# Layer 0's experts: an over-full expert changes places with number 17, which runs two blocks on one load of its weights

## The chip, the cores and the metric

The kernel runs on one core of a Trainium2 chip. The metric is the device time of one execution in microseconds (us), as the median of three runs. TensorE (PE) does the matmuls, VectorE (DVE), ScalarE (ACT) and GpSimd (POOL) the rest; SyncE (SP) issues most of the transfers from HBM.

## The reference

A trunk of two layers on 256 latent and 256 context tokens of width 1024. Each layer is a mixer (attention and a state-space scan in layer 0) with a hierarchical mixture of 32 experts behind it. Layer 0's experts see all 512 tokens, layer 1's the 256 latent ones. All is in fp32:

```python
g_prob = softmax(h @ wg + bg)                     # 4 groups of 8 experts
g_gate, g_sel = top_k(g_prob, 1)
e_top, e_idx = top_k(logits of the chosen group, 2)
gate = g_gate * softmax(e_top)
expert = g_sel * 8 + e_idx                        # two experts for each token
...
y[e] = (silu(x @ w1[e]) * (x @ w3[e])) @ w2[e]    # 1024 -> 512 -> 1024
out[token] += gate * y
```

The inputs are drawn with a fixed seed. Worked out from them with the reference's own router, layer 0's 1024 assignments fall on the 32 experts as in the first list, layer 1's 512 as in the second:

```
69 29 42 22 24 49 41 24 33 38 22 30 30 41 34 24 37 41 28 38 45 35 36 28 28 31 20 35 23 18 10 19
1 14 7 9 5 8 8 0 29 8 21 41 6 18 37 22 27 8 7 11 16 36 21 6 12 11 21 9 53 16 9 15
```

## The kernel before

Tokens of one expert are gathered into a block of 64 slots (`CAP`). `moe` runs the experts in order, four to a group; `nt` is the number of token tiles of 128, 4 in layer 0 and 2 in layer 1. For each expert six loads of 1 MiB (halves of `w1` and `w3`, and `w2`) are issued by SP into a ring of twelve buffers (tiles `ringw` and `raw`). PE multiplies (`a`, in `expert_up`), ACT and DVE apply silu and the gate (`sa`, `expert_gate`), PE turns the product (`hp`, `expert_turn`) and multiplies by `w2` (`py`, `expert_down`). The result is split into `yh` (ACT) and `yl` (DVE), and for each pair of experts eight combine steps bring it back to the tokens: PE `pcm`, DVE `ym`, and the add to `S` on POOL or DVE in turn. These steps wait in the list `todo`, those that fetch tokens in `steps`; `fill(n)` issues n of them between the matmuls of the next expert, so the order on PE is written out by hand.

Where a token goes is worked out on DVE. `dest` is its slot among the first 64 of each expert. `route_rest` numbers the overflow blocks, makes `odest` (the slot with overflow counted) and `ov`, a row of integers: the expert of each overflow block, and at the end how many blocks the loop has to run. A group's one-hots (`two`, made from `dq`) select its tokens: PE forms gates and row numbers with them (`pgs`), DVE casts the numbers to `ix`, POOL fetches the `rows` with an indirect load, and PE turns them to `xg`.

The first overflow block of layer 0 is block 32 of the same sequence (`nb = 33`); its expert comes from a register that SP loads from `ov` (L1024), and its gates are made in `block_gates` (`ovd`, `ovg`, eight of each for 512 tokens). Any further block is run by a loop behind the sequence, with a barrier of all engines at either end:

```python
n = nc.values_load(ov[0:1, NOV + 1:NOV + 2], ...)       # L1847
with tc.For_i(0, n, 1) as i:                            # L1848
    e = nc.values_load(ov[0:1, ds(i + 1, 1)], ...)
    oh = self.onehots(ep, nt, self.odest, base, CAP)
    xg, steps = self.turn_rows(ep, self.block_rows(ep, nt, oh), CAP)   # nt == 4
    for step in steps: step()
    c = dict(oh=oh, sl=slice(0, CAP), gs=self.block_gates(ep, nt, base))
    ...
    self.block(ep, layer, tiles, e, xg[:, :, 0, :], c)
```

`block` loads the expert's weights, runs its matmuls and its eight combine steps with nothing else between them. Here n = total - min(total, 1), total being the number of overflow blocks.

Of the kernel before, what the change touches and what calls it, by code (L numbers as in the profile page):

```python
# [32 lines left out]
DM = 1024  # L33
# [5 lines left out]
NOV = 16  # L39

# [27 lines left out]
class Trunk:  # L68
# [338 lines left out]
    def moe_tiles(self, nt):  # L407
        mp = self.moep
        self.h2h = mp.tile([128, nt, 8, 128], F32R, name="h2h")
        self.h2l = mp.tile([128, nt, 8, 128], F32R, name="h2l", tag="h2l", bufs=1)  # L410
        self.lg = mp.tile([128, nt, 36], F32, name="lg")
        self.dest = mp.tile([128, nt, 2], F32, name="dest")
        self.odest = mp.tile([128, nt, 2], F32, name="odest")
        self.gate = mp.tile([128, nt, 2], F32, name="gate")
        self.ov = mp.tile([128, 32], I32, name="ov")

# [573 lines left out]
    def moe(self, layer, tiles):  # L990
# [4 lines left out]
        with ExitStack() as es:  # L995
            with self.pool("exp", "right") as ep:
# [56 lines left out]

                nb = 33 if nt == 4 else 32


                for e in range(nb + 1):
                    cur = cur if e == 0 else begin(e) if e < nb else None
                    if e == 32 and cur:
                        C[16] = B['c']  # L1060
                    elif e % 2 == 0 and e < 32:
                        C[e // 2] = dict(oh=ohs[e // 4], sl=slice(64 * (e % 4), 64 * (e % 4) + 128))
                    if cur and e:
                        self.expert_up(cur, 0)
                    fill(2)

                    fill({1: 0, 2: 2, 3: 2}.get(e, 2 if e > 28 or e % 4 == 1 else 1) if nt == 4 else 2 if e > 28 else 1, steps)
                    if prev:
                        self.expert_turn(prev)
                    if cur:  # L1070
                        self.expert_up(cur, 1)
                    fill(2)
                    if e == 0:
                        gates(0)
                    if e % 4 == 2 and e < 28 and nt == 2:
                        gates(e // 4 + 1)
                    if cur:
                        cur['gs'] = cur['gs']()
                        self.expert_gate(cur)
                    if prev:  # L1080
                        k = (e - 1) % 2
                        c = C[(e - 1) // 2]
                        if k == 0 and e < 33:
                            self.combine_turn(ep, nt, c)
                        self.expert_down(prev, c, k)
                        if k or e == 33:
                            todo += self.combine_steps(ep, tiles, c, CAP if e == 33 else 128)
# [56 lines left out]
    def turn_rows(self, ep, rows, n):  # L1144
# [3 lines left out]
        xg = ep.tile([128, 8, 4, 64], F32, name="xg", bufs=2)  # L1148
# [25 lines left out]
    def group_gates(self, ep, nt, oh, e, rows=None):  # L1174

        gs = ep.tile([64, 4], F32, name="gs", bufs=3)
        for i in range(2):
            pg = self.ps([128, 2, 33], "pgs")
            for t in range(nt):
                self.mmp(pg.rearrange("p a b -> p (a b)"), oh[:, t, 128 * i:128 * i + 128], self.gdr[:, t].rearrange("p a b -> p (a b)"),  # L1180
                         start=(t == 0), stop=(t == nt - 1))
# [410 lines left out]
    def route_rest(self, nt):  # L1592
# [23 lines left out]
        gd = self.ep.tile([128, nt, 32], F32, name="gd")  # L1616
# [8 lines left out]
        V.tensor_copy(self.gdr[:, :, 1, 32], self.tok[:, 0:nt])  # L1625
        V.tensor_scalar(ge, R, float(4 * NSLOT), None, op0=OP.is_ge)
# [14 lines left out]
        inc = inc[1][:, 16:48]  # L1641
        adj = rp.tile([128, 32], F32, name="adj")
        V.tensor_tensor(adj, inc, nov, OP.subtract)
        V.tensor_tensor(adj, adj, self.iota[:, 0:32], OP.subtract)
        V.tensor_scalar(adj, adj, float(CAP), float(NSLOT - CAP - 4 * NSLOT), op0=OP.mult, op1=OP.add)
        V.tensor_tensor(ge, ge, bc(adj), OP.mult)
        V.tensor_tensor(R, R, ge, OP.add)
        self.pick(self.odest, 0, nt, V)
        le = self.ym(self.ep, nt).rearrange("p (b e) -> p b e", e=32)
        V.tensor_tensor(le, inc[:, None, :].to_broadcast([128, NOV, 32]),  # L1650
                        self.iota[:, 0:NOV][:, :, None].to_broadcast([128, NOV, 32]), OP.is_le)
        eid = rp.tile([128, 32], F32, name="eid")
        V.memset(eid, 0.0)
        V.tensor_reduce(eid[:, 0:NOV], le, AX.X, OP.add)
        V.tensor_scalar(eid[:, 0:NOV], eid[:, 0:NOV], 31.0, None, op0=OP.min)

        V.tensor_scalar(eid[:, NOV:NOV + 1], inc[:, 31:32], 1.0, None, op0=OP.min)
        V.tensor_tensor(eid[:, NOV + 1:NOV + 2], inc[:, 31:32], eid[:, NOV:NOV + 1], OP.subtract)
        V.tensor_copy(self.ov, eid)

# [17 lines left out]
    def onehots(self, ep, nt, dest, base, n):  # L1678

        V = self.nc.vector  # L1680
        oh = self.oh_tile(nt)
# [86 lines left out]
    def expert_down(self, E, c, k):  # L1768
# [3 lines left out]
        w = self.wload(E['w2'])  # L1772
# [12 lines left out]
    def block_gates(self, ep, nt, base):  # L1785
# [3 lines left out]
        for t in range(nt):  # L1789
            for k in range(2):  # L1790
                d = ep.tile([128, 1], F32, name="ovd", bufs=2)
# [4 lines left out]
                og = ep.tile([128, CAP], F32, name="ovg", bufs=2)  # L1796
# [6 lines left out]
    def block_first(self, ep, nt):  # L1803
# [3 lines left out]
        def begin():  # L1807
            if nt == 4:
                B['oh'] = self.onehots(ep, nt, self.odest, float(NSLOT), CAP)
# [148 lines left out]
```

## Time and profile before

| | |
|---|---|
| median of 3 runs | 1798.81 us (1796.29 to 1799.51) |
| profiled execution | 1799.8 us |
| its span | 1797.9 us |
| mean granted clock of TensorE | 0.966 |
| busy share of the span | PE 92%, DVE 53%, ACT 29%, POOL 16% |
| moved by DMA | 536.15 MB, mean 298 GB/s |

All times in the rows below are counted from the start of the span. Layer 0's experts take the stretch from about 560 to 1091. A row of a timeline gives start, duration, engine, line of the kernel and operation, with `out<-in` by the kernel's names; a bracket holds the idle time of the engine just ahead of it and what ended it.

### The profile page before, as it was taken

How to read it: one execution, taken by the hardware profiler on the slowest of the kernel's cores; microseconds unless marked ns; L12 is line 12 of the kernel's file. 1: busy time of each engine (PE TensorE's matmuls, PEld its weight loads, DVE VectorE, ACT ScalarE, POOL GpSimd, SP SyncE). 2: the span in 40 equal slices, each digit the busy share in tenths (PEclk: the TensorE clock that was granted, in tenths of full speed). 3: DMA queues.
4: the chain of work that ended last, by engine and by line, in shares of the span. 5: the costliest groups of instructions: out<-in, count | busy, mean ns of one | idle time of the engine just before them, and what ended most of it. 6: DMA issues, size and time to landing. Idle time of an engine off the chain costs nothing. (4 is left out here: it accounts for less than half of the span.)

```text
span 1797.9 us, 21742 instructions
## 1 busy us (share of the span) xinstructions
PE 1662.9 (92%) x8093; PEld 861.7 (48%) x8093; DVE 949.2 (53%) x2065; ACT 517.1 (29%) x1003; POOL 284.0 (16%) x257
## 2 busy tenths in 40 slices
PE   6999999999998999999999995989989999999994
PEld 2665565667455444443434334955544444444441
DVE  2354569777676345554555457865553343333425
ACT  2433446444212111111111113477231111111111
POOL 2210000000012412211221124240020010100101
PEclk8999999999998999999999996999989999999998
DMA  9555465654627999999999961352469999999994
GB/s 327 213 203 196 155 190 170 233 199 115 241 74 271 419 420 420 420 421 420 420 421 421 412 270 63 120 211 86 188 258 421 421 421 421 420 421 421 421 421 162
DMA packets 103070, 536.15 MB, mean 298 GB/s; under 512 B 20656, under 2 KB 24752, under 8 KB 49328
## 3 DMA queue, kind: packets, MB, share of 16 engines
q1 hardware_dynamic: 98032, 519.69, 73.7%
q0 software_dynamic: 4928, 15.02, 2.4%
q8 instruction: 66, 1.08, 0.2%
q14 instruction: 44, 0.36, 0.1%
HBM read 531.36 MB, written 3.30 MB: 297 GB/s over the span
## 5 line engine op out<-in xcount | busy, mean ns | idle before, releaser
L197 PE MATMUL a<-ringw,xg 128*64 128x512 f32 x1584 | 368.8, 607 | 2.0 <-DVE ovbase L1843 1.7
L197 PEld LDWEIGHTS a<-ringw,xg 128*64 128x64 f32 x1584 | 113.5, 140 | 211.6 <-issue 203.5
L1206 DVE TENSOR_TENSOR ym<-pcm,mod 128x512 f32<-128x512 f32 x136 | 90.6, 688 | 167.0 <-PE pcm L197 162.2
L1783 DVE TENSOR_TENSOR yl<-py,yh 64x512 fp32r<-64x512 f32 x130 | 89.5, 688 | 163.3 <-ACT yh L1782 161.7
L1782 ACT ACTIVATE yh<-py 64x512 fp32r<-64x512 f32 x130 | 76.8, 591 | 275.1 <-PE py L197 224.3
L1207 POOL TENSOR_TENSOR S<-S,ym 128x512 f32<-128x512 f32 x68 | 86.4, 1271 | 387.3 <-DVE ym L1206 387.3
L197 PE MATMUL py<-ringw,g 128*64 128x512 f32 x640 | 146.1, 597 | 0.0
L197 PE MATMUL a<-raw,xg 128*64 128x512 f32 x496 | 115.3, 603 | 1.8 <-DMA raw<-in_moe_w_dram 1.8
L216 PE MATMUL adaps<-adw,cs 128*32 128x512 f32 x384 | 96.2, 643 | 14.9 <-DMA adw<-in_ada_w_dram 14.9
L105 PE MATMUL pfm<-hTh,wh 128*128 128x512 f32 x256 | 105.0, 412 | 2.8 <-ACT hTh L99 2.7
L1207 POOL TENSOR_TENSOR S<-S,two 128x512 f32<-128x512 f32 x32 | 40.9, 1278 | 407.7 <-DVE two L1206 407.7
L106 PE MATMUL pfm<-hTh,wl 128*128 128x512 f32 x256 | 103.2, 403 | 0.0
L107 PE MATMUL pfm<-hTl,wh 128*128 128x512 f32 x256 | 100.7, 398 | 0.0
L1757 ACT ACTIVATE sa<-a 64x512 f32<-64x512 f32 x65 | 38.4, 591 | 208.9 <-PE a L197 208.9
L197 PE MATMUL pcm<-yh,ohT 128*128 128x512 f32 (+1 forms) x200 | 91.5, 458 | 6.6 <-DVE ym L1206 4.5
L197 PE MATMUL py<-raw,g 128*64 128x512 f32 x400 | 91.3, 598 | 0.5 <-ACT g L1766 0.5
L1206 DVE TENSOR_TENSOR two<-pcm,S 128x512 f32<-128x512 f32 x64 | 42.7, 689 | 92.1 <-PE pcm L197 91.6
L197 PEld LDWEIGHTS py<-ringw,g 128*64 128x64 f32 x640 | 43.7, 136 | 81.2 <-issue 74.2
L197 PEld LDWEIGHTS pcm<-yh,ohT 128*128 128x128 f32 (+1 forms) x200 | 38.2, 191 | 91.4 <-issue 64.8
L197 PE MATMUL pcm<-yl,ohT 128*128 128x512 f32 (+1 forms) x200 | 80.8, 404 | 0.6 <-DVE yl L1783 0.6
L1758 DVE SCALAR_TENSOR_TENSOR sa<-sa,gs,a 64x512 f32<-64x512 f32 x64 | 47.9, 749 | 56.5 <-ACT sa L1757 55.1
L1207 DVE TENSOR_TENSOR S<-S,ym 128x512 f32<-128x512 f32 x68 | 66.5, 978 | 1.8
(519 smaller groups left out, 2754.5 us busy)
## 6 DMA issues: line engine op xcount, KB each, us to landing
ringw<-in_moe_w_dram SPq DMA_DIRECT2D x278, 1024.0 KB, 18.8
raw<-in_moe_w_dram SPq DMA_DIRECT2D x112, 1024.0 KB, 18.4
adw<-in_ada_w_dram SPq DMA_DIRECT2D x96, 512.0 KB, 5.3
raw<-in_w_in_dram SPq DMA_DIRECT2D x18, 1024.0 KB, 8.2
bc<-atd SPq DMA_DIRECT2D x16, 512.0 KB, 6.7
raw<-in_w_out_dram SPq DMA_DIRECT2D x4, 1024.0 KB, 5.6
raw<-in_o_w_out_dram SPq DMA_DIRECT2D x4, 1024.0 KB, 5.9
bias<-in_rpb_dram SPq DMA_DIRECT2D x8, 256.0 KB, 3.8
```

The costliest lines, as they stand in the source:

```text
L105: mm(out, ah, bh, start=start, stop=False)
L106: mm(out, al, bh, start=False, stop=False)
L107: mm(out, ah, bl, start=False, stop=stop)
L197: return self.tc.keep_in_program_order(self.nc.tensor.matmul(*args, **kw))
L216: self.nc.tensor.matmul(p[32 * g:32 * g + 32, :], self.cs[:, j, :], w[:, (g - g0) * 512:(g - g0 + 1) * 512], start=(j == 0), stop=(j == 7))
L1206: nc.vector.tensor_tensor(m, p, self.rows5[t // 2][:, k], OP.mult)
L1207: (nc.gpsimd if i % 2 == 0 else nc.vector).tensor_tensor(S[:, t, k], S[:, t, k], m, OP.add)
L1757: self.nc.scalar.activation(s, a[0:64, :], AF.Silu)
L1758: self.nc.vector.scalar_tensor_tensor(s, s, E['gs'], a[64:128, :], op0=OP.mult, op1=OP.mult)
L1782: nc.scalar.activation(c[h][0][r], py[q], AF.Copy)
L1783: V.tensor_tensor(c[h][1][r], py[q], c[h][0][r], OP.subtract)
```

## The change

In layer 0 the sequence has 32 experts again, and number 17 is run on two blocks with one load of its weights (`twice`). If one of the experts 4 to 31 is over-full, `swap` exchanges it with number 17: the slots, the gates and, through the row `perm`, the weights that are loaded, so the loads of experts 4 to 31 take their address from a register. The overflow block that 17 runs is the exchanged expert's; the others are numbered behind it. If none of them is over-full, `z` is 1, nothing is exchanged, and all overflow blocks are left to the loop. The 33rd load is dropped. The groups' one-hots behind the first take `odest`, which now comes out of `route_rest` with the exchange in it. The second block's tokens are prepared at experts 9 to 12, with one buffer for `ovd` and `ovg`, and all combine steps in `todo` are issued at e = 19.

```diff
-                    ohs[q] = self.onehots(ep, nt, self.dest, 256.0 * q, 256) if q else self.oh0
+                    ohs[q] = self.onehots(ep, nt, self.odest if nt == 4 else self.dest, 256.0 * q, 256) if q else self.oh0
...
                 def begin(e):
-                    if e == 32:
-                        at = nc.values_load(self.ov[0:1, 0:1], engines=[mybir.EngineType.SP], min_val=0, max_val=31)
-                        return self.expert_begin(ep, layer, None, B['xg'][:, :, 0, :], lambda: B['gs'], load=self.expert_at(layer, at))
-                    return self.expert_begin(ep, layer, e, X[e // 4][:, :, e % 4, :], lambda: gs[e // 4][:, e % 4:e % 4 + 1])
+                    load = None
+                    if nt == 4 and e >= 4:
+                        at = nc.values_load(self.perm[0:1, e:e + 1], engines=[mybir.EngineType.SP], min_val=4, max_val=31)
+                        load = self.expert_at(layer, at)
+                    return self.expert_begin(ep, layer, e, X[e // 4][:, :, e % 4, :], lambda: gs[e // 4][:, e % 4:e % 4 + 1], load)
...
-                nb = 33 if nt == 4 else 32
+                nb, twice = 32, None
...
-                    fill({1: 0, 2: 2, 3: 2}.get(e, 2 if e > 28 or e % 4 == 1 else 1) if nt == 4 else 2 if e > 28 else 1, steps)
+                    fill({1: 0, 2: 2, 3: 2, 9: 3, 10: 3, 11: 3, 12: 3}.get(e, 2 if e > 28 or e % 4 == 1 else 1) if nt == 4 else 2 if e > 28 else 1, steps)
...
-                    fill(2)
+                    fill(len(todo) if twice and e == TWICE + 2 else 2)
...
+                        if prev is twice:
+                            c, k, n = B['c'], 0, CAP
...
-                    if e == 27:
+                    if e == (8 if nt == 4 else 27):
...
+                    if e == TWICE and nt == 4:
+                        twice = dict(cur, xg=B['xg'][:, :, 0, :], gs=B['gs'])
+                        self.expert_up(twice, 0)
+                        fill(2)
+                        self.expert_turn(prev)
+                        self.expert_up(twice, 1)
+                        fill(2)
+                        self.expert_gate(twice)
+                        self.expert_down(prev, C[e // 2], 1)
+                        todo += self.combine_steps(ep, tiles, C[e // 2])
+                        twice['w', 2] = prev['w', 2]
+                        prev = twice
...
+        if nt == 4:
+            self.swap(adj, nov, total, gd, nt)
...
+        if nt == 4:
+            V.tensor_copy(eid[:, NOV + 1:NOV + 2], total[:, 1:2])
...
+    def swap(self, adj, nov, total, gd, nt):
+        nc, V, rp = self.nc, self.nc.vector, self.rp
+        it = self.iota[:, 0:32]
+        mx, z, x, dl = (rp.tile([128, 1], F32, name=n) for n in ("swm", "swz", "swx", "swd"))
+        df = rp.tile([128, 32], F32, name="swf")
+        ix, A, Bm, pm = (self.D[:, 1, i] for i in range(4))
+        V.memset(ix[:, 0:4], 0.0)
+        V.scalar_tensor_tensor(ix[:, 4:32], nov[:, 4:32], 1.0, it[:, 4:32], op0=OP.min, op1=OP.mult)
+        V.tensor_reduce(mx, ix, AX.X, OP.max)
+        V.tensor_scalar(z, mx, 0.0, None, op0=OP.is_equal)
+        V.scalar_tensor_tensor(x, z, float(TWICE), mx, op0=OP.mult, op1=OP.add)
+        V.tensor_scalar(adj, adj, z, None, op0=OP.add)
+        V.tensor_tensor(total[:, 1:2], total[:, 0:1], z, OP.add)
+        V.tensor_scalar(total[:, 1:2], total[:, 1:2], -1.0, None, op0=OP.add)
+        V.tensor_scalar(A, it, x, None, op0=OP.is_equal)
+        V.scalar_tensor_tensor(df, it, float(TWICE), A, op0=OP.is_equal, op1=OP.subtract)
+        V.tensor_scalar(dl, x, float(-TWICE), None, op0=OP.add)
+        self.move = rp.tile([128, 32], F32, name="swv")
+        V.tensor_scalar(self.move, df, dl, None, op0=OP.mult)
+        V.tensor_tensor(pm, self.move, it, OP.add)
+        V.tensor_copy(self.perm, pm)
+        V.tensor_scalar(self.move, self.move, float(CAP), None, op0=OP.mult)
+        V.tensor_scalar(A, df, -1.0, 0.0, op0=OP.mult, op1=OP.max)
+        V.tensor_scalar(Bm, df, 0.0, None, op0=OP.max)
+        bc = lambda a: a[:, None, :].to_broadcast([128, nt, 32])
+        gx, g17 = (rp.tile([128, nt], F32, name=n) for n in ("swgx", "swg17"))
+        t = self.D[:, 0]
+        V.tensor_tensor(t, gd, bc(A), OP.mult)
+        V.tensor_reduce(gx, t, AX.X, OP.add)
+        V.tensor_copy(g17, gd[:, :, TWICE])
+        V.tensor_tensor(ix, df, df, OP.mult)
+        V.tensor_scalar(ix, ix, -1.0, 1.0, op0=OP.mult, op1=OP.add)
+        V.tensor_tensor(gd, gd, bc(ix), OP.mult)
+        for m, g in ((A, g17), (Bm, gx)):
+            V.tensor_tensor(t, bc(m), g[:, :, None].to_broadcast([128, nt, 32]), OP.mult)
+            V.tensor_tensor(gd, gd, t, OP.add)
+        self.gdr = self.ep.tile([128, nt, 2, 33], F32R, name="gdr1")
+        nc.scalar.activation(self.gdr[:, :, 0, 0:32], gd, AF.Copy)
+        V.tensor_tensor(self.gdr[:, :, 1, 0:32], gd, self.gdr[:, :, 0, 0:32], OP.subtract)
...
-            E['w', i] = [self.whalf(w[:, 4 * i:4 * i + 4]) for w in E['w13']]
+            if ('w', i) not in E:
+                E['w', i] = [self.whalf(w[:, 4 * i:4 * i + 4]) for w in E['w13']]
...
-                d = ep.tile([128, 1], F32, name="ovd", bufs=2)
+                d = ep.tile([128, 1], F32, name="ovd", bufs=1)
...
-                og = ep.tile([128, CAP], F32, name="ovg", bufs=2)
+                og = ep.tile([128, CAP], F32, name="ovg", bufs=1)
```

VectorE (DVE) where the experts start, before: `dq` and the one-hots `two` of group 1 are among the first rows behind `dest`.

```order
L1684 TENSOR_SCALAR dq<-dest 128x8 x2
L1619 TENSOR_TENSOR gd<-gd,raw 128x128
L1731 COPY xg<-pg 128x512
L1843 MEMSET ovbase 128x1
L1636 SCALAR_TENSOR_TENSOR raw<-raw 128x32
L1662 TENSOR_SCALAR two_4472<-iota,dq 128x256 x4
L1636 SCALAR_TENSOR_TENSOR raw<-raw 128x32
L1623 TENSOR_TENSOR gdr<-gd,gdr 128x4x32
L1663 SCALAR_TENSOR_TENSOR two_4472<-iota,dq,two_4472 128x256 x4
```

And now, at the end of `route_rest`:

```order
L1202 TENSOR_REDUCE gs<-pgs 64x1 x2
L1684 TENSOR_SCALAR raw<-raw 128x16
L1606 TENSOR_REDUCE odest<-raw 128x2x4
L1839 SCALAR_TENSOR_TENSOR sa<-sa,gs,a_4366 64x512
L1685 TENSOR_SCALAR raw<-raw 128x16
L1764 TENSOR_SCALAR dq<-odest 128x8 x2
L1876 TENSOR_SCALAR ovd<-odest 128x1
L1202 TENSOR_REDUCE gs<-pgs 64x1 x2
L1692 CAST ov<-raw 128x32
L1742 TENSOR_SCALAR two_4509<-iota,dq 128x256 x4
L1880 TENSOR_SCALAR ovg<-iota,ovd,gate 128x64
L1743 SCALAR_TENSOR_TENSOR two_4509<-iota,dq,two_4509 128x256 x4
```

The one-hots of group 1 moved from a place ahead of `route_rest`'s small rows to one behind `odest`, with `sa` of expert 0, `gs` and `ov` ahead of them; between the copy of `xg` from `pgb` and `odest` there are by the order some 19 rows more than before. On PE the `pgs` of group 1 stands where it stood, ahead of expert 1's `a`.

PE where expert 18 is run down, before (`a` of expert 19, two combine steps of a `yh` and a `yl` row each, `poT`, and `py`):

```order
L197 MATMUL a_6205<-raw,xg 64x512 x8
L197 MATMUL pcm<-yh,ohT 128x512
L197 MATMUL pcm<-yl,ohT 128x512
L197 MATMUL pcm<-yh,ohT 128x512
L197 MATMUL pcm<-yl,ohT 128x512
L201 MATMUL poT<-ident,two_5528 128x128 x4
L197 MATMUL py_6277<-raw,g 64x512 x8
```

And now, at e = 19, where twenty `pcm` rows in pairs of `yh` and `yl` stand between `a` and `poT`, all alike:

```order
L199 MATMUL a_6556<-raw,xg 64x512 x8
L199 MATMUL pcm<-yh,ohT 128x512
L199 MATMUL pcm<-yl,ohT 128x512
L199 MATMUL pcm<-yh,ohT 128x512
L199 MATMUL pcm<-yl,ohT 128x512
...
L203 MATMUL poT<-ident,two_5716 128x128 x4
L199 MATMUL py_6676<-raw,g 64x512 x8
```

Ten combine steps stand where two stood; behind them there are none on PE until e = 21. On SP 28 register reads of `perm` are added (a TENSOR_LOAD and two small instructions each), most of them among the first loads behind expert 1's.

## Rows read from the trace of the kernel before

**Rows 1.** The table of stretches: for each, time and count per engine, granted clock, DMA share, GB/s.

```profile
600.00:660.00 60.00, 57.89 (x276) 24.66 (x270) 29.69 (x51) 11.02 (x20) 11.10 (x9) 1.00 1.01 421
...
1062.00:1092.00 30.00, 21.21 (x69) 9.44 (x68) 24.13 (x32) 3.35 (x6) 11.45 (x9) 0.79 0.05 20
```

**Rows 2.** PE's waits from 600 to 1060: total us, times, longest.

```profile
PE pg L201 <- DVE ym L1206: 8.4, 23, 0.4
PE pgs L197 <- DVE gs L1186: 6.1, 6, 1.0
PE pgs L197 <- DVE ovg L1797: 1.5, 3, 1.1
```

**Rows 3.** Tile `ringw`, SP's issues between 976 and 979.5, and their time to landing.

```profile
L430 SPq DMA_DIRECT2D ringw<-in_moe_w_dram x2: 328/328/328, 976.6 to 979.0; - x2
...
DMA to landing us min/median/max: 19.7/19.7/19.8
```

**Rows 4.** PE's timeline from 1000: start, duration, line, operation.

```profile
1001.51 1.89 PE L197 MATMUL a<-ringw,xg 128*64 128x512 f32 x8
```

**Rows 5.** DVE's timeline at the end of layer 0's experts.

```profile
1087.15 1.27 DVE L1207 TENSOR_TENSOR S<-S,ym 128x512 f32<-128x512 f32 x1
...
1089.65 1.26 DVE L1207 TENSOR_TENSOR S<-S,ym 128x512 f32<-128x512 f32 x1
1093.08 4.84 DVE L843 BATCH_NORM_STATS2 lnst<-S 128x6 f32<-128x512 f32 x8 [2.17 <-issue]
```

**Rows 6.** DVE's timeline at their start; in brackets the idle time before.

```profile
561.78 1.14 DVE L1662 TENSOR_SCALAR two<-iota,dq 128x256 fp32r<-128x256 f32 x4
...
563.14 1.66 DVE L1663 SCALAR_TENSOR_TENSOR two<-iota,dq,two 128x256 fp32r<-128x256 f32 x4
...
568.24 1.10 DVE L1640 TENSOR_TENSOR raw<-raw 128x32 f32<-128x32 f32 x5
...
573.46 0.34 DVE L1186 TENSOR_REDUCE gs<-pgs 64x1 f32<-64x2 f32 x2 [1.26 <-PE pgs L197]
```

**Rows 7.** Tile `rows`: the indirect loads of token rows.

```profile
DMA to landing us min/median/max: 8.1/10.2/12.4
```

**Rows 8.** PE's timeline at block 32's gates.

```profile
1007.28 0.39 PE L197 MATMUL pgs<-one,ovg 128*64 128x2 f32 x4 [0.86 <-DVE ix L1134]
...
1009.44 0.50 PE L197 MATMUL pgs<-one,ovg 128*64 128x2 f32 x4 [0.21 <-DVE ovg L1797]
1010.15 0.50 PE L197 MATMUL pgs<-one,ovg 128*64 128x2 f32 x4 [0.20 <-DVE ovg L1797]
```

**Rows 9.** PE's timeline in the steady part.

```profile
826.91 3.65 PE L197 MATMUL a<-raw,xg 128*64 128x512 f32 x16
830.50 0.50 PE L197 MATMUL pcm<-yh,ohT 128*128 128x512 f32 x1
...
831.53 0.60 PE L201 MATMUL poT<-ident,two 128*128 128x128 f32 x4
```

**Rows 10.** PE's timeline at the start of the experts.

```profile
561.81 3.68 PE L197 MATMUL a<-ringw,xg 128*64 128x512 f32 x8 [1.71 <-DVE ovbase L1843]
...
576.34 0.60 PE L197 MATMUL pgs<-gdr,two 128*128 128x66 f32 x4 [1.79 <-DVE gs L1186]
...
578.20 5.15 PE L197 MATMUL a<-ringw,xg 128*64 128x512 f32 x16
```

**Rows 11.** PE's timeline behind the last `a`.

```profile
1066.33 0.50 PE L197 MATMUL pcm<-yh,ohT 128*128 128x512 f32 x1 [0.69 <-ACT yh L1782]
...
1070.51 3.65 PE L197 MATMUL py<-ringw,g 128*64 128x512 f32 x16
```

**Rows 12.** Tile `ov`: SP's register reads at the start (ns min/median/max, start).

```profile
L1024 SPq TENSOR_LOAD <-ov x1: 479/479/479, 574.6 to 574.6; - x1
L1847 SPq TENSOR_LOAD <-ov x1: 278/278/278, 575.4 to 575.4; - x1
```

**Rows 13.** SP's waits from 560 to 600.

```profile
SPq L430 <- PE a L197: 30.3, 5, 13.9
```

More of the change, by code (lines that the diff above doesn't have):

```diff
@@ L39 @@
 NOV = 16
+TWICE = 17
 class Pinned:
@@ L415, in moe_tiles @@
         self.ov = mp.tile([128, 32], I32, name="ov")
+        self.perm = mp.tile([128, 32], I32, name="perm")
     def rload(self, src):
@@ L1080, in moe @@
                     if prev:
[L1081 removed]
+                        k, n = (e - 1) % 2, 128
                         c = C[(e - 1) // 2]
[L1083 to L1084 removed]
+                        if prev is twice:
+                            c, k, n = B['c'], 0, CAP
+                        if k == 0:
+                            self.combine_turn(ep, nt, c, n)
                         self.expert_down(prev, c, k)
[L1086 to L1087 removed]
+                        if k or n == CAP:
+                            todo += self.combine_steps(ep, tiles, c, n)
                     if e == 0:
@@ L1142, in next_rows, with turn_rows @@
         return self.rows[:, self.rows_n]
-    def turn_rows(self, ep, rows, n):
+    def turn_rows(self, ep, rows, n, xg=None):
         nc, V = self.nc, self.nc.vector
         k = n // 64
-        xg = ep.tile([128, 8, 4, 64], F32, name="xg", bufs=2)
+        xg = ep.tile([128, 8, 4, 64], F32, name="xg", bufs=2) if xg is None else xg
         def step(jp):
@@ L1615, in route_rest @@
         g2, ge = (rp.tile([128, nt, 32], F32) for _ in range(2))
-        gd = self.ep.tile([128, nt, 32], F32, name="gd")
+        gd = self.ym(self.ep, nt)[:, 0:32 * nt].rearrange("p (t e) -> p t e", t=nt)
         V.tensor_tensor(gd, oh[:, 0], gate[:, :, 0:1].to_broadcast([128, nt, 32]), OP.mult)
@@ L1642, in route_rest @@
         adj = rp.tile([128, 32], F32, name="adj")
-        V.tensor_tensor(adj, inc, nov, OP.subtract)
+        V.tensor_scalar(adj, inc, inc[:, 31:32], -1.0, op0=OP.subtract, op1=OP.mult)
+        total = rp.tile([128, 2], F32, name="ovn")
+        V.tensor_copy(total[:, 0:1], inc[:, 31:32])
+        if nt == 4:
+            self.swap(adj, nov, total, gd, nt)
+        ends = rp.tile([128, 32], F32, name="ends")
+        V.tensor_tensor(ends, adj, nov, OP.add)
         V.tensor_tensor(adj, adj, self.iota[:, 0:32], OP.subtract)
@@ L1645, in route_rest @@
         V.tensor_scalar(adj, adj, float(CAP), float(NSLOT - CAP - 4 * NSLOT), op0=OP.mult, op1=OP.add)
+        if nt == 4:
+            V.tensor_tensor(adj, adj, self.move, OP.subtract)
         V.tensor_tensor(ge, ge, bc(adj), OP.mult)
         V.tensor_tensor(R, R, ge, OP.add)
+        if nt == 4:
+            V.tensor_tensor(R, R, bc(self.move), OP.add)
         self.pick(self.odest, 0, nt, V)
         le = self.ym(self.ep, nt).rearrange("p (b e) -> p b e", e=32)
-        V.tensor_tensor(le, inc[:, None, :].to_broadcast([128, NOV, 32]),
+        V.tensor_tensor(le, ends[:, None, :].to_broadcast([128, NOV, 32]),
@@ L1659, in route_rest @@
-        V.tensor_copy(self.ov, eid)
+        V.tensor_scalar(eid[:, 0:NOV], eid[:, 0:NOV], -1.0, 31.0, op0=OP.mult, op1=OP.add)
+        V.tensor_scalar(eid[:, 0:NOV], eid[:, 0:NOV], 0.0, None, op0=OP.max)
+        if nt == 4:
+            V.tensor_copy(eid[:, NOV + 1:NOV + 2], total[:, 1:2])
+        else:
+            V.tensor_scalar(eid[:, NOV:NOV + 1], total[:, 0:1], 1.0, None, op0=OP.min)
+            V.tensor_tensor(eid[:, NOV + 1:NOV + 2], total[:, 0:1], eid[:, NOV:NOV + 1], OP.subtract)
@@ L1771, in expert_down @@
         g = E['g']
-        w = self.wload(E['w2'])
+        if ('w', 2) not in E:
+            E['w', 2] = self.wload(E['w2'])
+        w = E['w', 2]
         py = self.ps([128, 512], "py2")
@@ L1808, in begin @@
             if nt == 4:
-                B['oh'] = self.onehots(ep, nt, self.odest, float(NSLOT), CAP)
+                B['oh'] = self.onehots(ep, nt, self.odest, float(NSLOT), CAP, ep.tile([128, nt, CAP], F32R, name="ohB"))
                 return
@@ L1814, in rows @@
         def rows():
-            B['xg'], B['steps'] = self.turn_rows(ep, self.block_rows(ep, nt, B['oh']), CAP)
+            B['xg'], B['steps'] = self.turn_rows(ep, self.block_rows(ep, nt, B['oh']), CAP,
+                                                 self.moep.tile([128, 4 * DM], F32, name="xgB", tag="h2h", bufs=1)[:, 0:512]
+                                                 .rearrange("p (j a s) -> p j a s", j=8, a=1))
         def rest():
```

21 lines of the change are left out of this document (10 added, 11 removed).

## Prediction

> **What bounds the kernel now.** The change touches the stretch from 560 to 1091 us, layer 0's experts. I read the table of stretches first. In the steady part the DMA share is 1.01 and 421 GB/s move, while PE is busy 57.89 of 60 [rows 1]: two resources look full at once. Which of them binds is read from PE's waits. From 600 to 1060 PE waited 8.4 us for VectorE's `ym`, 6.1 for `gs` and 1.5 for `ovg`; the two rows left out are DVE's as well, 1.1 together [rows 2]. No row names a DMA. So the weight stream is just fast enough and is never waited for, and PE, one expert after the other, sets the time. How close it is: the tightest pair of loads is issued at 976.6 and 979.0 and takes at most 19.8 [rows 3], so it lies in SBUF by 998.8; its matmuls start at 1001.51 [rows 4], 2.7 later. In the last 30 us of the stage 20 GB/s move and PE is busy for 21.2 [rows 1]: there the combine steps of the last experts run at VectorE's pace.
>
> **The change, part by part.** *The dropped load.* Six loads of 1 MiB (6.29 MB) at 421 GB/s [rows 1] are 14.9 us of DMA time. PE waits for none of it, and the sequence keeps 33 blocks (17 twice in place of number 32), so PE's work stays. Worth 0; the bound on the other side, -14.9, is a rival below.
>
> The Trainium skill ("Perfetto Trace Analysis", Identifying the Most-Contended Engine) says to optimize the resource with the highest use first, here the DMA; by it the sum would hold -14.9 for this term. PE's waits speak against it: the trace shows a full resource that nobody waits for.
>
> *What the exchange does with these inputs.* swap() sets candidates 0 to 3 to zero and takes the largest index among the over-full experts from 4 to 31. The counts of layer 0 (above) have one expert over 64: number 0, with 69; the next has 49. So `mx` is 0, `z` is 1, the exchange is the identity, and expert 17's second block holds no token but is computed all the same. The overflow numbers are shifted by one, and the loop's count is total + z - 1 = 1 + 1 - 1 = 1. Before, expert 0's second block was block 32 in the overlapped sequence and the loop's count was 0: the last add ends at 1089.65 + 1.26 = 1090.91, only the skipped loop's barrier follows, and the next layer's first VectorE work starts at 1093.08 [rows 5]. After, layer 0 computes 32 blocks, an empty one, and one in the loop that stands alone behind a barrier.
>
> *The price of one turn of the loop.* Nothing in the trace runs it, so I build it from like rows in the order of its code, with nothing overlapped but its weights:
> - one more all-engine barrier like the 2.17 at the skip [rows 5]: 2.2 (1 to 4.4);
> - eight one-hot operations of width 64, `pgs`, `ix`: the 256-wide ones take 1.14 and 1.66 for four [rows 6], 2.8 in all; narrower here, but with PE and `ix` behind them, an estimate of 2.9 (2 to 4);
> - the gather of the rows, 8.1 to 12.4 from issue to landing [rows 7]; for 64 rows on an idle DMA the smallest, 8.1;
> - eight transposes and their copies, an estimate of 2.2 (2 to 4);
> - the gates: eight `ovg`, each with a matmul. With two buffers two of them take 1010.15 - 1009.44 = 0.71 [rows 8], 0.35 each. With one buffer PE's read and VectorE's write alternate; I take about twice that, 0.78: 6.2 (2.8 to 8);
> - `ovgs` and `poT`: 1.1 (1 to 2);
> - 32 rows of `a`: sixteen take 3.65 in the steady part [rows 9]; behind a wait eight take 3.68 [rows 10], half the rate. So 7.3 at one level of the clock and 14.7 at the other; PE idles through most of the loop, so a mix, 9.8;
> - activation, gate and `hp`, from engine to engine, an estimate of 2.4 (2 to 3); `py` 3.65 [rows 11];
> - eight combine steps: VectorE's own `S` adds, one for two steps, start 2.50 apart (1087.15 to 1089.65) [rows 5], so 10.0 for eight, with the first wait of 0.69 [rows 11], its `yl` and the last add 12.5 (11 to 15).
>
> The six loads start at the barrier too; at 421 GB/s they take 15 and land before the gates end at about 21, so they hide. Sum 51; all low bounds give 41, all high ones 71.
>
> The Trainium skill ("Runtime: NRT & Kernel Launch", Instruction fetch mechanics) says that a taken branch out of the fetched window makes its engine wait for a fetch. No row here shows a turn of a loop; it would move the 51 toward its top.
>
> *The start.* Group 1's one-hots (1.14 + 1.66) started at 561.78, beside expert 0's matmuls [rows 6]. They now need `odest`, which by the order stands behind some 19 more small VectorE rows. Five such rows take 1.10 [rows 6], so +3.8; DVE idled 1.26 ahead of the `gs` at 573.46 [rows 6], right before `odest`, so 2.5 of it is seen and `odest` ends near 576.4. Then `sa`, `dq`, `gs` and `ov` (about 1.6) and the one-hots with an `ovg`: the last at about 581. PE's `pgs` of group 1, at 576.34 before, waits for them, its last pair ends at about 581.7, and only then can expert 1's `a` start, 578.20 before [rows 10]: +3.5 (2 to 6, the upper end with another stretch of half clock behind the longer wait). All of PE's work is queued behind it, so it is paid in full.
>
> *SP's register reads.* 29 reads, 28 of them new. The two shown start 0.8 apart [rows 12], so 23 us of SP in all. SP waited 30.3 us there for PE to free ring buffers, up to 13.9 at once [rows 13], and a read needs no buffer. Worth 0; if that cover is gone, a rival.
>
> *One buffer for `ovd` and `ovg`.* Block B's gates move to experts 9 to 12. Seven intervals × (0.78 - 0.35) = +3.0, less the 0.86 that PE waited there for `ix` [rows 8], which other work now fills: +2.2 (-1 to +4).
>
> *The flush at e = 19.* Ten combine steps in a row on PE. In the steady part two steps take 831.53 - 830.50 = 1.03 [rows 9]; at VectorE's pace two take 2.5 [rows 5]. Ten would lose 7.4; the first few find free buffers: +4.5 (0 to 7.4).
>
> *The tail.* From the end of the last `py` (1070.51 + 3.65 [rows 11]) to 1090.91 there were 12 steps in 16.8; now 8: 0.7 + 0.7 + 10.0 + 1.8 = 13.2. The four steps cost 4 × 0.515 = 2.1 further ahead: -1.5 (-3 to 0).
>
> Without the loop: 3.5 + 0 + 2.2 + 4.5 - 1.5 = +8.7 (-2 to +17). With it about +59.7.
>
> **The rivals.** (a) *The loop does not run*: the chip's router would have to give expert 0 five assignments fewer. The skipped loop before fits one overflow block or none, so the trace alone doesn't settle it; the counts do. Then +8.7 alone, about 1807. (b) As (a), and flush, gates and start find cover: within 0.2% (3.6 us), about what timing this kernel can tell. (c) *The dropped load pays*, the faster side: if PE keeps pace with the stream, 14.9 come back, about 1784 where the loop isn't run either. It decides from the point where the margin of 2.7 is gone and PE waits for weights; [rows 2] show no such wait. Should it pay and the loop run, the time is about 1843, inside my range. (d) *SP's reads starve the stream at the start*: if half of their 23 came through, 1870; SP's 30.3 of waiting speaks against it.
>
> **How the numbers follow.** The sum is made on the profiled execution, 1799.8, which is 1.0 above the median of 1798.8: 1799.8 + 8.7 + 51 - 1.0 = 1858. The low ends, -2 and 41, give 1838, the high ones, +17 and 71, give 1887; as a range 1836 to 1886. The loop runs: 0.87, nearly all of it inside the range, (d) too. (a) 0.06, (b) 0.03, (c) 0.04. Slower 0.93, same 0.03, faster 0.04.
>
> **What the profile would show.** Right: behind the last `S` add of the sequence one more block, with a gather and six loads at its start, 32 `a` matmuls, and PE idle for most of some 50 us. Group 1's `pgs` waits several us for `two` at the start; the DMA share falls at the end of the stage, while PE's waits still name DVE. Wrong: no `a` between the last add and layer 1 (a); PE waits gone that named a DMA (c), or such a wait come at the start (d); a turn far below 41, where its engines overlap more than the order of the code says.

## The result and the profile after

The changed kernel takes 1847.7 us (median of 4 runs, 1846.69 to 1848.99) where the kernel before took 1797.8 beside it: the ratio is 1.028, with an interval of 1.0265 to 1.0296, so about 50 us slower. Its profiled execution has a span of 1847.1. The prediction was 1858, with a range of 1836 to 1886.

The table of stretches of the changed kernel answers to [rows 1]:

```profile
600.00:660.00 60.00, 57.88 (x272) 24.96 (x270) 31.68 (x61) 11.04 (x20) 11.43 (x10) 1.00 1.01 420
...
1062.00:1092.00 30.00, 26.60 (x104) 11.54 (x100) 20.79 (x29) 4.92 (x9) 8.92 (x7) 0.93 0.77 289
1092.00:1150.00 58.00, 27.01 (x107) 13.16 (x106) 32.49 (x78) 9.61 (x17) 15.54 (x12) 0.65 0.21 72
```

The steady part is as full as before. What is new is the last row: 58 us, the last 14 of them already the next layer's, in which PE is busy for 27, at a mean granted clock of 0.65, and 72 GB/s move. PE's waits from 600 to 1060 answer to [rows 2]:

```profile
PE pg L203 <- DVE ym L1222: 7.4, 20, 0.4
PE pgs L199 <- DVE gs L1202: 5.3, 6, 1.0
PE pgs L199 <- DVE ovg L1880: 4.4, 7, 1.6
PE pcm L199 <- DVE ym L1222: 2.9, 5, 0.8
PE pg L203 <- DVE xg L1177: 1.2, 1, 1.2
PE pg L203 <- DMA rows<-h2d,ix: 0.9, 1, 0.9
```

Again no row names a load of weights; waits for `ovg` grew from 1.5 to 4.4 and `pcm` waits for `ym` have come up. DVE's timeline at the end of layer 0's experts answers to [rows 5]:

```profile
1093.20 1.26 DVE L1223 TENSOR_TENSOR S<-S,ym 128x512 f32<-128x512 f32 x1
1094.38 0.15 DVE L1766 TENSOR_TENSOR dq<-odest,ovbase 128x8 f32<-128x8 f32 x1
...
1135.06 1.26 DVE L1223 TENSOR_TENSOR S<-S,ym 128x512 f32<-128x512 f32 x1
1136.72 4.84 DVE L846 BATCH_NORM_STATS2 lnst<-S 128x6 f32<-128x512 f32 x8 [0.41 <-DVE S L1223]
```

Between the last add of the sequence (1093.20 + 1.26 = 1094.46) and the next layer's first VectorE work lie 42.3 us, where the kernel before had 2.2. Behind the add comes a `dq` made from `ovbase`: the loop's first instruction, with no idle time ahead of it. The count of the loop is 1, as forecast. PE in that turn:

```profile
1095.88 0.76 PE L199 MATMUL pgs<-gdr,two 128*64 128x2 f32 x4 [3.67 <-DVE two L1743]
1100.88 0.70 PE L203 MATMUL pg<-ident,rows 64*128 64x64 f32 x4 [4.25 <-DMA rows<-h2d,ix]
...
1102.37 0.37 PE L199 MATMUL pgs<-one,ovg 128*64 128x2 f32 x2
...
1107.83 0.37 PE L199 MATMUL pgs<-one,ovg 128*64 128x2 f32 x2 [0.41 <-DVE ovg L1880]
...
1109.43 8.16 PE L199 MATMUL a<-ringw,xg 128*64 128x512 f32 x32
...
1120.29 3.65 PE L199 MATMUL py<-ringw,g 128*64 128x512 f32 x16 [0.53 <-ACT g L1847]
1124.64 0.50 PE L199 MATMUL pcm<-yh,ohT 64*128 64x512 f32 x1 [0.69 <-ACT yh L1865]
```

Read from above: PE waits for the one-hots, then for the rows' gather; the gate matmuls (one `ovg` each) stand 0.78 apart; 32 `a` rows take 8.16 and nothing waits for weights. Two more rows, SP's issues and the time of `rows` to landing in that stretch, show a gather that is quick and weights that are there:

```profile
1076.73 4.24 SPq L433 DMA_DIRECT2D ringw<-in_moe_w_dram  x6
```

```profile
DMA to landing us min/median/max: 3.7/3.7/3.7
```

SP went into the loop 18 us ahead of DVE and issued the six loads from 1076.73 to 1080.5; the slowest took 16.5 to landing, so they had landed when POOL started the gather at 1097.1. The gather took 3.7 to landing, where [rows 7] had 8.1 at the least. That the free DMA is the reason is tested below, with two turns of the loop.

### The profile page after: what moved, and what is told of

Its sections match the earlier page's. It is cut to its first block, busy times and chain, and to the rows that moved or that the text cites. A ratio compares the mean times of both kernels' runs of the same rounds, so it can differ in the third digit from the quotient of the medians.

```text
span 1847.1 us, 22468 instructions
## 1 busy us (share of the span) xinstructions
PE 1693.2 (92%) x8193; PEld 875.1 (47%) x8193; DVE 974.0 (53%) x2147; ACT 521.2 (28%) x1011; POOL 289.5 (16%) x262
## 5 line engine op out<-in xcount | busy, mean ns | idle before, releaser
L1222 DVE TENSOR_TENSOR ym<-pcm,mod 128x512 f32<-128x512 f32 x144 | 95.7, 687 | 157.8 <-PE pcm L199 152.9
L1223 POOL TENSOR_TENSOR S<-S,ym 128x512 f32<-128x512 f32 x72 | 91.7, 1273 | 416.6 <-DVE ym L1222 416.6
L199 PE MATMUL py<-ringw,g 128*64 128x512 f32 x656 | 150.0, 597 | 0.5 <-ACT g L1847 0.5
L199 PE MATMUL pcm<-yh,ohT 128*128 128x512 f32 (+1 forms) x208 | 97.0, 466 | 10.6 <-DVE ym L1222 7.5
L199 PE MATMUL pcm<-yl,ohT 128*128 128x512 f32 (+1 forms) x208 | 85.7, 412 | 0.8 <-DVE yl L1866 0.8
L1223 DVE TENSOR_TENSOR S<-S,ym 128x512 f32<-128x512 f32 x72 | 71.4, 992 | 2.1
```

The lines of the kernel that those rows point to most:

```text
L199: return self.tc.keep_in_program_order(self.nc.tensor.matmul(*args, **kw))
L1222: nc.vector.tensor_tensor(m, p, self.rows5[t // 2][:, k], OP.mult)
L1223: (nc.gpsimd if i % 2 == 0 else nc.vector).tensor_tensor(S[:, t, k], S[:, t, k], m, OP.add)
```

## The experiments

**The loop's count set to 0** (expert 0's second block is left out).

```diff
-            V.tensor_copy(eid[:, NOV + 1:NOV + 2], total[:, 1:2])
+            V.memset(eid[:, NOV + 1:NOV + 2], 0.0)
```

> The change with the loop's count set to 0, so expert 0's second block is left out. Theory (the one turn of the loop is the loss): the trace of the change has 42.3 us from the last S add of the sequence to layer 1's first VectorE work, where the kernel before has 2.2, so 40 come back: 1847.7 - 40 = 1807 to 1809, still 9 to 11 above the kernel before. Rival (the sequence itself became slower through register addresses, the empty block and the flush, and most of the loop was covered): less than half comes back, 1828 or more. Rival (the dropped load pays, and only the loop hid it): below 1798.

Measured: 1807.2, ratio to the kernel before 1.0046 (1.0029 to 1.0063). 40.5 us came back (42 by the two ratios), what the trace showed; 5 to 11 are left for everything else in the change.

**Reversed labels**: the exchange takes place, and the loop is not run.

```diff
-        load = load or (lambda n: self.I[n][layer, e])
+        load = load or (lambda n: self.I[n][layer, 31 - e])
...
-        V.tensor_copy(self.perm, pm)
+        V.tensor_scalar(self.perm, pm, -1.0, 31.0, op0=OP.mult, op1=OP.add)
...
-    o['router'] = f(np.concatenate([g('moe_wg'), g('moe_we')], 2).reshape(...))
+    o['router'] = f(np.concatenate([g('moe_wg')[..., ::-1], g('moe_we')[..., ::-1]], 2).reshape(...))
...
```

> The change with the experts' labels counted from 31 down (router columns reversed, weights of label l read from expert 31 - l), so that the over-full expert has label 31, the exchange with 17 takes place and the loop's count is 0; the whole result is computed. Theory: what the exchange moves costs nothing by itself, and the time is that of the loop's count set to 0: 1807 to 1809. Rival (an exchange that takes place costs more than an identity, through other weights or a longer chain to the gates): 1812 or more. Rival (the dropped load pays once the second block is real): below 1798.

Measured: 1806.8, ratio 1.0047 (1.0028 to 1.0065), the same as with the loop's count at 0. An exchange that takes place costs what an identity costs, within these intervals. It also shows the change as it was meant, with 32 loads and 33 blocks: it is still slower than the kernel before.

**33 loads again** (reversed labels): the second block drops the weights it was given and loads its own.

```diff
-                        twice = dict(cur, xg=B['xg'][:, :, 0, :], gs=B['gs'])
+                        twice = {k: v for k, v in dict(cur, xg=B['xg'][:, :, 0, :], gs=B['gs']).items() if not isinstance(k, tuple)}
...
-                        twice['w', 2] = prev['w', 2]
```

> The kernel with reversed labels, but the second block of 17 loads its expert's weights once more, so that 33 loads are made as before. Theory (the DMA stream is full but PE waits for none of it): the time of reversed labels, within 3 us. Rival (PE keeps pace with the stream, so each load is worth its DMA time): 6 loads of 2.5 us more, +15.

Measured: 1811.5 (1805.66 to 1816.34), ratio 1.0058 (1.0036 to 1.0080) against 1.0047; the medians are 4.6 apart, outside the 3 of the theory, the ratios 2. Two later pairs ask the same: 1.0044 against 1.0030, where the exchange is left out as well, and 1.0264 against 1.0246. The kernels with 33 loads come out 0.1 to 0.2% slower, 2 to 3 us, with intervals that overlap in each pair; 15 is excluded. No wait for weights shows on PE in layer 0's experts in any of them.

The traces of this pair show that the load isn't what separates them. From the first `a` to the last add, layer 0's experts take 535.2 with 32 loads and 542.6 with 33, but the difference has arisen before expert 17 is reached, where the two kernels are alike; behind it nothing more is added. Part of it stands at the gates of a group, with 32 loads and then with 33:

```profile
756.72 0.60 PE L199 MATMUL pgs<-gdr,two 128*128 128x66 f32 x4 [0.70 <-DVE gs L1202]
...
757.87 3.65 PE L199 MATMUL a<-ringw,xg 128*64 128x512 f32 x16
```

```profile
762.42 1.03 PE L199 MATMUL pgs<-gdr,two 128*128 128x66 f32 x4 [0.70 <-DVE gs L1201]
...
764.05 6.05 PE L199 MATMUL a<-ringw,xg 128*64 128x512 f32 x16
```

Behind the same wait of 0.70 the sixteen `a` take 3.65 at a granted clock of 1.00 in one execution and 6.05 at 0.60 in the other. In the second pair the traces' difference, 3.7 at expert 16, is also there before expert 17 and stays 3.7 to the end. In the third, PE's waits for gathers are 42.8 with 33 loads and 38.5 with 32; whether the load makes that difference stays open.

**Two turns of the loop**, the second over a block without tokens.

```diff
-            V.tensor_copy(eid[:, NOV + 1:NOV + 2], total[:, 1:2])
+            V.tensor_scalar(eid[:, NOV + 1:NOV + 2], total[:, 1:2], 1.0, None, op0=OP.add)
```

> The change with one more turn of the loop, over an overflow block that holds no token. Theory: a turn costs what the first one shows, about 42 us from its start to its last S add; its weights are issued at the back edge and not ahead of the barrier, but land in 15 to 20 while gather, gates and a take 15 to 23, so +42 to +48: 1890 to 1896. Rival (the weights of the first turn were hidden by being issued 17 us early; without that the a matmuls wait for them): +50 or more, with a PE wait of a for a DMA.

Measured: 1906.1, +58.4 in one run. DVE's timeline at the back edge (the jump from the end of one turn to the start of the next) and at the end, and PE's in the second turn:

```profile
1137.58 1.26 DVE L1223 TENSOR_TENSOR S<-S,ym 128x512 f32<-128x512 f32 x1
1143.84 0.17 DVE L1766 TENSOR_TENSOR dq<-odest,ovbase 128x8 f32<-128x8 f32 x1 [5.00 <-PEq L1935]
...
1192.26 1.26 DVE L1223 TENSOR_TENSOR S<-S,ym 128x512 f32<-128x512 f32 x1
```

```profile
1145.35 0.76 PE L199 MATMUL pgs<-gdr,two 128*64 128x2 f32 x4 [8.78 <-DVE two L1743]
1155.20 0.70 PE L203 MATMUL pg<-ident,rows 64*128 64x64 f32 x4 [9.09 <-DMA rows<-h2d,ix]
...
1163.75 9.56 PE L199 MATMUL a<-ringw,xg 128*64 128x512 f32 x32
...
1176.02 5.12 PE L199 MATMUL py<-ringw,g 128*64 128x512 f32 x16 [0.54 <-ACT g L1847]
```

From the first turn's last add (1137.58 + 1.26 = 1138.84) to the second's (1192.26 + 1.26 = 1193.52) it is 54.7, where the first turn took 41.8. The 12.9 are in the rows: 5.0 idle at the back edge, 9.09 instead of 4.15 for the gather, which now shares the DMA with six loads issued at the same time, and `a` and `py` longer by 1.4 and 1.5, at mean granted clocks of 0.74 and 0.71 where the first loop's turn in the changed kernel had 0.87 and 1.00. Both theories missed: the size is the rival's, but PE doesn't wait for weights; the loads delay the gather.

**Gate operands in one tile** (reversed labels; all eight products, then all eight matmuls).

```diff
...
-                og = ep.tile([128, CAP], F32, name="ovg", bufs=1)
...
+        og = self.ym(ep, nt)
+        for j in range(2 * nt):
+            t, k = divmod(j, 2)
+            V.tensor_scalar(og[:, 64 * j:64 * j + 64], self.iota[:, :CAP], d[:, t, k:k + 1], self.gate[:, t, k:k + 1], ...)
+        for j in range(2 * nt):
+            self.mmp(pg, og[:, 64 * j:64 * j + 64], self.one2, ...)
...
```

> The kernel with reversed labels; the eight gate operands of a block stand side by side in one tile (a ym buffer) and not in one ovg buffer after the other, and one subtraction makes all offsets. Theory: the waits of pgs for ovg were 4.4 us in layer 0 and 2.8 in layer 1, each with some 1.5 of half clock behind it, and the kernel before had about 2.6 and 1.5 of them: about 6 less than reversed labels, 1800 to 1802. Rival (the wait only moves, to ym, which the combine steps need): within 2 us of reversed labels, 1805 to 1809.

Measured: 1808.2, ratio 1.0048 (1.0029 to 1.0067), no gain; the rival holds. PE at the gates in this kernel:

```profile
735.08 1.75 PE L199 MATMUL pgs<-one,ym 128*64 128x2 f32 x16 [2.59 <-DVE ym L1879]
...
737.87 4.78 PE L199 MATMUL a<-raw,xg 128*64 128x512 f32 x16
```

One wait of 2.59 stands in place of seven, and the burst behind it still takes 4.78 where 3.65 is the steady value [rows 9]. VectorE finishes the operands too late, however they are stored.

**Spread steps** (reversed labels; no flush).

```diff
-                    fill(len(todo) if twice and e == TWICE + 2 else 2)
+                    fill(3 if twice and TWICE + 2 <= e < TWICE + 10 else 2)
```

> The kernel with reversed labels; in place of all combine steps at e = 19, one more step per expert in the eight experts from 19 on. Theory: the ten steps took 11.4 us of PE's time where ten in the steady part take 5.2, and 1.3 of half clock came behind, so 7 to 8 less than reversed labels: 1799 to 1800. Rival (the steps wait for VectorE wherever they stand): within 2 us of reversed labels.

Measured: 1804.8, ratio 1.0032 (1.0022 to 1.0043): 2 of the 7 to 8. Behind the flush's place the next expert's `a` starts at 888.1 and not at 898.2, so its 10 us are gone there; but from there to the last expert's first `a` PE takes 169.4 and not 161.9. Eight steps cost 7.4 in their new places, where eight of the 0.515 from [rows 9] are 4.1. Most of the other 3.3 stands at one place, the first gates behind the moved steps:

```profile
894.74 0.60 PE L199 MATMUL pgs<-gdr,two 128*128 128x66 f32 x4 [1.34 <-DVE gs L1202]
...
895.89 5.35 PE L199 MATMUL a<-ringw,xg 128*64 128x512 f32 x16
```

With reversed labels alone this wait is 0.58 and the burst 3.65, 2.5 less together.

**Both mends together.**

> Reversed labels, the gates in one tile and the spread steps together: the change as meant, with 32 loads and no loop. Theory: the two gains add, 1807 - 6 - 7.5 = 1793 to 1795, 5 below the kernel before, from the shorter tail (8 steps in 12.4 us where 12 took 16.8) and cheaper gates. Rival (they overlap, or the state of the clock gives them back): 1797 to 1801, no faster than before.

Measured: 1804.5, ratio 1.0030 (1.0019 to 1.0041). The gains do not add to a faster kernel; the rival's side is nearer, and it was too hopeful too.

**The same order, no exchange, 33 loads.** The block behind expert 17 takes its weights by a register from `ov`, swap() isn't called, the groups' one-hots take `dest` again.

```diff
-                        twice = dict(cur, xg=B['xg'][:, :, 0, :], gs=B['gs'])
+                        at = nc.values_load(self.ov[0:1, 0:1], engines=[mybir.EngineType.SP], min_val=0, max_val=31)
+                        twice = self.expert_begin(ep, layer, None, B['xg'][:, :, 0, :], B['gs'], self.expert_at(layer, at))
...
```

> As the one before, with the same order of blocks, gates and steps, but without any exchange: the block behind expert 17 is the first overflow block with a load of its own by a register, 33 loads as before, labels not reversed, group one-hots from dest. Theory (the exchange and the dropped load are worth nothing, the order of the blocks is all): within 3 us of the one before. Rival (the dropped load pays): 8 to 15 above it, 1802 or more. Rival (the exchange's VectorE rows ahead of group 1 cost): 3 or more below it.

Measured: 1807.6, ratio 1.0044 (1.0029 to 1.0059). Leaving out the exchange and loading again changes 0.14%, inside the intervals, and not to the faster side: the exchange is not what makes these kernels slower than the one before. The new order of the blocks, with its gates and its tail, is what is left.

**Gate operands one step ahead** (reversed labels and spread steps; the products issued a step before their matmuls, in a tile of their own).

```diff
...
+        def ops():
+            B['og'] = self.gate_ops(ep, nt, float(NSLOT))
...
         def rest():
-            B['gs'] = self.block_gates(ep, nt, float(NSLOT))
+            B['gs'] = self.block_gates(ep, nt, B['og'])
...
-        return B, [begin, rows, rest] + turn if nt == 4 else [begin] + turn + [rest]
+        return B, [begin, rows, ops, rest] + turn if nt == 4 else [begin] + turn + [ops, rest]
```

> Reversed labels and spread steps, with the gate operands of a block (VectorE) made one step ahead of their matmuls (PE), in a tile of their own. With both in one step PE still waited 2.6 us for them in layer 0 and 2.5 in layer 1, each with 1.5 of half clock behind. Theory (that wait is what is left of the gates' cost): 5 to 7 below the kernel with both mends, 1798 to 1800. Rival (the clock falls for another reason, or the block's other steps cost the time): within 2 us of it, 1803 to 1806.

> The one before with 33 loads: the second block of 17 loads its weights again. Theory (the dropped load is worth nothing to PE): within 2 us of it. Rival (it is worth something, as the two pairs so far leave open, 4.6 and 3.1 more with 33 loads): 3 to 5 more. Rival (worth its DMA time): 15 more.

Measured: 1843.6 (1.0246) and with 33 loads 1844.2 (1.0264). The first is far above its theory and its rival alike; between the two are 0.7 by the medians and 3 by the ratios. The waits of PE from 600 to 1130 in the first of them:

```profile
PE pg L203 <- DMA rows<-h2d,ix: 38.5, 8, 8.8
```

My reading: with one more entry the list of token-fetching steps ran one step late for the rest of the stage, so each group's gather was issued too close to the transposes that need it. The next run tests it.

**The same with one more step taken at expert 10.**

```diff
-                    fill({1: 0, 2: 2, 3: 2, 9: 3, 10: 3, 11: 3, 12: 3}.get(e, 2 if e > 28 or e % 4 == 1 else 1) if nt == 4 else 2 if e > 28 else 1, steps)
+                    fill({1: 0, 2: 2, 3: 2, 9: 3, 10: 4, 11: 3, 12: 3}.get(e, 2 if e > 28 or e % 4 == 1 else 1) if nt == 4 else 2 if e > 28 else 1, steps)
```

> Reversed labels, spread steps, gate operands one step ahead, and one step more taken from the list of token-fetching steps at expert 10, so that the groups behind it fetch their rows as early as without the added step. In the kernel without it PE waited 38.5 us for rows, 8 times. Theory (those waits came from the list running one step late, nothing else): they go, and the gain for the gates shows: 1797 to 1800, 5 to 7 below the kernel with the gates in one step, and 7 to 10 above the kernel before with the same mend of its gates (1790.5). Rival (the order of blocks is then as good as the one before): 1789 to 1793. Rival (the exchange delays the rows themselves): still above 1820.

Measured: 1796.4 (12 runs, 1792.58 to 1803.95), ratio 0.9989 (0.9974 to 1.0004): no row of PE's waits in layer 0 names a gather any more, so the reading holds, and the mend of the gates shows, 8 below both mends. PE at the gates:

```profile
733.91 1.09 PE L199 MATMUL pgs<-one,xgB 128*64 128x2 f32 x16
...
736.00 3.65 PE L199 MATMUL a<-raw,xg 128*64 128x512 f32 x16
```

No wait at the matmuls, and the burst behind them at full rate. (`xgB` names the tile that the operands share with the second block's tokens.) PE has a new wait in this kernel, 3.89 for a `dq` at the third group's gates (623.93); why is open.

**The kernel before with the same mend**, none of the change in it.

> The kernel before, without any of the change, with the gate operands made one step ahead in a tile of their own, in both layers. Theory: PE's waits there were 2.6 us in layer 0 with 1.25 of half clock, and 1.9 in layer 1: 3 to 5 below the kernel before, 1794 to 1796. Rival (the waits move to the next thing that VectorE owes PE): within 2 us of it.

Measured: 1790.5, ratio 0.9966 (0.9953 to 0.9978), below the kernel before by 8.2 in the medians and 6.1 in the ratio (4.0 to 8.5), more than forecast. By the two traces the stretch of layer 0's gates gave 5.6, of which the tail took 1.1 back, and layer 1's gates 1.6: 6.1 in all. Layer 1's gates, in the kernel before and then in this one:

```profile
1758.90 0.50 PE L197 MATMUL pgs<-one,ovg 128*64 128x2 f32 x4 [1.46 <-DVE ovg L1797]
```

```profile
1749.44 0.63 PE L197 MATMUL pgs<-one,ogB 128*64 128x2 f32 x8
...
1751.52 3.65 PE L197 MATMUL a<-ringw,xg 128*64 128x512 f32 x16
```

The 1.46 that PE waited there before is gone. With the same mend in both, the change as it was meant (1796.4) is still slower than the kernel before (1790.5), 5.9 in the medians and 0.2% in the ratios: so mended it gains nothing over the order that it replaced.

## Why the prediction was right

The decisive step was the one on the inputs: expert 0 is the only over-full one and the exchange cannot take it, so the loop runs once. The kernel with its count at 0 shows this turn to be 40.5 of the 50. The median lies 10 below the 1858, inside the range; the turn alone was priced 11 too high.

Where a size was off:

- **The turn of the loop**, 51 forecast, 42.3 - 2.2 = 40.1 in the trace. Three terms of that sum were too large. The extra barrier (2.2) isn't there: the entry costs DVE nothing, and the exit 0.41 where the skip took 2.17, about 4 in all. The section on the kernel before speaks of a barrier of all engines at either end of the loop; at the entry there is none, the engines pass the loop's first branch one after another, SP at 1075.5, ACT at 1084.3, PE at 1091.4, POOL at 1093.3 and DVE at 1093.9. The gather took 4 with its wait and not 8.1, since the loads had landed; the step "the six loads start at the barrier too" failed, SP was in the loop long before. The `a` rows took 8.16 and not 9.8. The steps (12.4 to 12.5) were right, and the gates too (0.78 per pair, as taken); that it was 0.78 and not the 0.70 of twice 0.35 was luck. The second turn, which has a back edge and its loads beside the gather, took 54.7: the sum was nearer to that one.
- **The start**, +3.5 forecast. PE at the start answers to [rows 10]:

```profile
559.04 1.94 PE L199 MATMUL a<-ringw,xg 128*64 128x512 f32 x8 [0.49 <-DVE ovbase L1930]
...
572.82 1.52 PE L199 MATMUL pgs<-gdr,two 128*128 128x66 f32 x4 [3.27 <-DVE two L1743]
...
575.88 5.26 PE L199 MATMUL a<-ringw,xg 128*64 128x512 f32 x16
```

The wait of `pgs` for the moved one-hots is there, 3.27, as forecast. From the first `a` to expert 1's it is 16.8, and in the kernel before 16.4, so +0.4 against the one trace of it. But there the first burst ran at a granted clock of 0.50 (3.68), and that isn't the one-hots' doing: in the two later kernels whose one-hots stand where they stood, the one without the exchange and the kernel before with its gates mended, it takes 1.94 at 1.00. The latter's start:

```profile
558.40 1.94 PE L197 MATMUL a<-ringw,xg 128*64 128x512 f32 x8 [1.62 <-DVE ovbase L1859]
...
572.41 6.06 PE L197 MATMUL a<-ringw,xg 128*64 128x512 f32 x16
```

Here it is 14.0, as in the other one, and against these the changed kernel's 16.8 is +2.8, near the forecast; the shorter wait ahead of its first `a`, 0.49 for 1.62, gives 1.1 back. The +0.4 is luck of the one trace, not a mistake of the term.
- **SP's reads**, 0 forecast. SP's waits answer to [rows 13], and the reads of `perm` to [rows 12]:

```profile
SPq L433 <- PE a L199: 18.3, 5, 10.0
```

```profile
L1028 SPq TENSOR_LOAD <-perm x28: 262/262/494, 564.9 to 583.2; - x28
```

28 reads of mostly 262 ns took about 12 us of SP's waiting for buffers, and PE waits for no load. Right.
- **The gates**, +2.2 forecast. PE at layer 0's and at layer 1's gates:

```profile
733.64 0.28 PE L199 MATMUL pgs<-one,ovg 128*64 128x2 f32 x2 [1.57 <-DVE ovg L1880]
...
739.82 5.21 PE L199 MATMUL a<-raw,xg 128*64 128x512 f32 x16
```

```profile
1805.00 0.28 PE L199 MATMUL pgs<-one,ovg 128*64 128x2 f32 x2 [1.57 <-DVE ovg L1880]
...
1808.30 5.16 PE L199 MATMUL a<-ringw,xg 128*64 128x512 f32 x16
```

The burst behind layer 0's gates in the kernel before:

```profile
1012.19 4.90 PE L197 MATMUL a<-raw,xg 128*64 128x512 f32 x16
```

Layer 0: 4.4 of waits where there were 2.6 (1.5 for `ovg` and the two rows left out), and behind them a burst 1.56 longer than the steady 3.65 where it was 1.25 longer: +2.1, right. But one buffer holds for layer 1 as well, which I left out: 2.8 of waits and not 1.5, and a burst of 5.16 and not 3.65, +2.8.
- **The flush**, +4.5 forecast, at most 7.4. PE at e = 19:

```profile
881.50 0.50 PE L199 MATMUL pcm<-yh,ohT 128*128 128x512 f32 x1
...
892.92 1.11 PE L203 MATMUL poT<-ident,two 128*128 128x128 f32 x4
893.97 4.94 PE L199 MATMUL py<-raw,g 128*64 128x512 f32 x16
```

From 881.50 to `poT` at 892.92 it is 11.4 for ten steps that cost 5.2 in the steady part, +6.3, and the `py` behind them takes 4.94 and not 3.65: 7.6.
- **The tail**, -1.5 forecast: 12.4 from the end of the last `py` to the last add, before 16.8, with the 2.1 paid elsewhere -2.3.

Without the loop these make +10.6 against 8.7, the runs with its count at 0 say +7.7 (5.2 to 11.3). So the small terms came out nearly right in sum, with a flush and layer 1 too cheap; how far others made up for that, one trace of each kernel can't say: in the pair with 32 and 33 loads a stretch in which the kernels are alike differed by more than 7.

- **The dropped load**, 0 forecast. The rule of the Trainium skill ("Perfetto Trace Analysis", Identifying the Most-Contended Engine), by which the fullest resource comes first, would have given 14.9. Three pairs gave 2 to 3, within their intervals, and in two of them the traces place it ahead of the load. The measurement stands against the rule here, as PE's waits had.

The rule on branches ("Runtime: NRT & Kernel Launch", Instruction fetch mechanics of the Trainium skill) can now be held beside a row: entering the loop left no gap on DVE, the back edge left 5.0. No packet of an instruction queue moves in that trace from 1136 to 1146, so no fetch is seen in these 5.0; in the 2.17 of the skipped loop one packet moves (1092.0 to 1092.5), but whose it is isn't shown.

## What to carry to other kernels

Work out from the inputs which branch a data-dependent kernel takes before pricing its parts: here one exclusion (experts 0 to 3) sent the only over-full expert to the path that nothing overlaps. A resource at full use is worth relieving only where its consumer waits for it. And where several engines hand over small operands, issue the producer's part a step ahead of the consumer's: that alone, on the kernel before, gave 6 to 8 us, where the change gave none; but an entry added to a list that is drained by count moves everything behind it.

## What the runs showed of the hardware

A gather of 64 rows landed after 3.6 us on a quiet DMA and after 8.6 beside six weight loads, in two turns of the same loop. A wait of PE can cost twice: behind the 2.59 for gate operands, sixteen `a` rows took 4.78 and behind no wait 3.65, at these granted clocks (table of stretches over the burst alone, first with one tile for the operands, then with operands a step ahead):

```profile
737.87:742.65 4.78, 4.78 (x18) 1.40 (x17) 0.00 (x0) 0.38 (x1) 0.00 (x0) 0.76 1.01 422
```

```profile
736.00:739.65 3.65, 3.65 (x18) 1.12 (x17) 0.40 (x2) 0.38 (x1) 0.00 (x0) 1.00 1.03 429
```

At 0.76 of the clock, between its two levels of 1.2 and 2.4 GHz, the burst lost 1.13 more, and with the wait taken away both came back. It doesn't have to be so: behind the same wait of 0.70 one execution ran its burst at 1.00 and another at 0.60, so what the clock takes behind a wait can't be read from a single trace.
